# Putting the weight split ahead of older work in the order of two engines

## The chip, the cores and the metric

The kernel runs on one core of one Trainium2 chip. The metric is device time in microseconds of one execution; lower is better.

## The reference

One layer of a model step, on a prompt of 512 tokens and 64 sample tokens (8 requests of 8), with float32 data. A combined projection of the normalised input feeds three branches, and the merged result goes through an output projection:

```python
hn = _rmsnorm(x, norm_g)
u, v, gate_a, z, xbc, dt_raw, q, gate_x, merge = split(hn @ w_in)
h_a = gelu(u) * spatial(layernorm(gelu(v))) * silu(gate_a)
xs, bm, cm = split(silu(causal_conv(xbc)))            # SSD branch
y, h_new = ssd(xs, softplus(dt_raw + dt_bias), -exp(a_log), bm, cm, h0)
h_b = gated_group_rmsnorm(y + d_skip * xs, z, ssd_norm_g)
h_x = mem_attention(q, mem_k, mem_v) * silu(gate_x)
m = g_a * (h_a @ w_proj_a) + g_b * (h_b @ w_proj_b) + g_x * (h_x @ w_proj_x)
return x + m @ w_out
```

The SSD branch is a state-space recurrence in chunks of 128 tokens, with 32 heads in 8 groups. The change lies in the stage that computes this branch.

## The kernel before

Tokens lie along the free dimension: 576 columns, the 512 of the prompt and the 64 samples, in two halves of 288. To multiply float32 data, every operand is split in two: `hi` is a rounded copy, `lo` is the difference. A product of 128 output rows is then three chains of matmuls per half, hi x hi, hi x lo and lo x hi, 24 matmuls of 288 columns per half (line 167).

The weights of a product are split right before use. `load_block` (line 130) reads a block of raw weights for two products into `wraw` (two buffers) on SyncE's queue. `wsplit` makes `whi` by a cast on ScalarE (line 98) and `wlo` by a subtraction on VectorE (line 99); both have two buffers. So the split of a product needs the buffers of the product two before it, and these are free when TensorE has done the last matmul of that one.

The SSD stage is a list of 72 such products, each a `Job` with three parts: `load`, `prep` (the split) and `half`, which runs for each half and also empties the PSUM buffer:

- `conv_job`: rows of xBC. The half is copied out of PSUM by ScalarE (lines 404, 408, 409), then a convolution of four taps follows, one on ScalarE (416) and three on VectorE (418), a tanh (420) and the gate, which makes `xs` or `C` (422, 426, 429); GpSimd copies a part of xs (432).
- `z_job`: the gate z. A tanh on ScalarE (462), then a multiplication on VectorE that reads the same PSUM buffer and makes `zs` (463).
- `gate_job`: merge gates, a tanh (732).
- `proj_job`: products of the finished branch (`hb`) with 512 rows of w_proj_b; a job makes two output row blocks, each in two blocks of 12 matmuls with a PSUM buffer of its own, added into `m_sb` on VectorE (755).

Three PSUM buffers (`acc`) serve all of these, in turn. Group g's jobs are the four conv products of group g + 1 (in the last group four gate products), two z products of group g and, from group 2 on, two proj products; four gate and eight proj products end the stage. In even groups from 2 on the order is conv, conv, conv, conv, z, proj, z, proj; in odd groups from 3 on conv, proj, conv, proj, conv, conv, z, z.

Between the halves stand the steps of the recurrence of group g, written out by hand in `steps(g)`: decays (e: 488, 489, 491), transposes and dt weighting (503 to 511), C x B (532, 533), the diagonal part (548, 559), the state (567 to 574), its part of the output (592 to 597), the sample states (644 to 659), and the gated norm of the group before (`gate_y`, `norm_y`: 685 to 705, with Ln in 701). They use the PSUM buffers `sps` (three) and `yps` (two). What a step leaves in PSUM is read by ScalarE or VectorE, and the buffer is free for a later step when that is done.

What sets the order: TensorE's instructions run as they are written (`manual_schedule`). For the other engines a planner steps through a modelled run of the program and gives each engine, whenever it is free, that ready instruction which has the lowest number. An instruction's number is counted up as the code is written. The result is a fixed queue for each engine, which it works through in order. The loop that writes the products:

```python
for j, h in units:
    ...
    i = at[id(j)]
    if h == 0:
        if i + 2 < len(jobs):
            jobs[i + 2].load()
        if i + 1 < len(jobs):
            jobs[i + 1].prep()
    j.half(h)
```

So at the start of a product the split of the next one is written, behind all steps written so far and ahead of the current product's own evacuations.

Of the kernel before, what the change touches and what calls it, by code (L numbers as in the profile page):

```python
# [42 lines left out]
def tile_hybrid_step(  # L43
# [156 lines left out]
    with ExitStack() as stb:  # L200
# [562 lines left out]
        with tc.manual_schedule(engines={mybir.EngineType.PE}):  # L763
# [63 lines left out]
            jobs = [u[0] for u in units if u[0] is not None and u[1] == 0]  # L827
# [4 lines left out]
            for j, h in units:  # L832
                if j is None:
                    for w_ in h:
                        w_()
                    continue
                i = at[id(j)]
                if h == 0:
                    if i + 2 < len(jobs):
                        jobs[i + 2].load()  # L840
                    if i + 1 < len(jobs):
                        jobs[i + 1].prep()
                j.half(h)

    lo_last[0] = True
# [648 lines left out]
```

## Time and profile before

| | |
|---|---|
| median of 3 runs | 1150.23 us (1148.32 to 1156.42) |
| profiled execution, its own time | 1151.22 us |
| span of the profiled execution | 1149.5 us |
| TensorE busy (PE) | 1099.6 us, 96% of the span |
| VectorE busy (DVE) | 781.9 us, 68% |
| ScalarE busy (ACT) | 622.1 us, 54% |
| GpSimd busy (POOL) | 37.7 us, 3% |

The span goes from the first to the last instruction of the program. Busy time is the union of an engine's instructions; a matmul's end is modelled, so neighbouring matmuls overlap by a little. The SSD stage runs from the start of the kernel to about 646 us. In the rows PE is TensorE's matmuls, PEld its weight loads, SPq SyncE's queue, and L99 line 99 of the kernel.

### The profile page before, as it was taken

The page shows a single profiled execution, that of the slowest core. Times are in us where ns is not written, and L with a number is a line of the kernel's source. Part 1 is how long each engine was busy: PE and PEld are TensorE (multiplying, and loading weights), DVE is VectorE, ACT ScalarE, POOL GpSimd, SP SyncE. Part 2 cuts the span into 40 slices and gives each one's busy share as a digit, 9 for nine tenths or more (in the row PEclk, how much of TensorE's full clock was granted, in tenths as well). Part 3 has the DMA queues.
Part 4 walks back from the last instruction along what each step waited for, and adds up shares of the span by engine and source line. Part 5 has one row for each costly group of instructions (what it writes and reads, how often), then busy time and mean ns, then how long its engine had stood idle before and what let it go on. Part 6 is the DMA issues. An engine that isn't in the chain of part 4 may idle for free.

```text
span 1149.5 us, 20445 instructions
## 1 busy us (share of the span) xinstructions
PE 1099.6 (96%) x8199; PEld 1024.1 (89%) x8199; DVE 781.9 (68%) x1450; ACT 622.1 (54%) x1294; POOL 37.7 (3%) x110
## 2 busy tenths in 40 slices
PE   5989999899999989989999999999999999999997
PEld 4989899799998989989999877899999999889776
DVE  5778787748787667866644644786875567775743
ACT  6456686766868456665553244344653236564421
POOL 3010010000000000000000000000000000000000
PEclk9999999999999999999999999999999999999999
DMA  6433544155352524425232525631262353465411
GB/s 190 128 82 111 156 116 138 59 159 145 98 156 84 155 88 126 126 70 169 88 115 95 190 74 165 193 111 52 96 222 101 130 180 102 121 183 197 152 47 73
DMA packets 160462, 144.90 MB, mean 126 GB/s; under 512 B 10160, under 2 KB 141264, under 8 KB 160368
## 3 DMA queue, kind: packets, MB, share of 16 engines
q1 hardware_dynamic: 137264, 126.12, 35.9%
q10 hardware_dynamic: 23104, 17.49, 4.8%
q8 instruction: 64, 1.05, 0.4%
q14 instruction: 30, 0.25, 0.1%
HBM read 124.13 MB, written 19.46 MB: 125 GB/s over the span
## 4 chain that ended last, share of the span: by engine, by line
PE 84%; DVE 6%; ACT 5%; DMA 3%; issue 1%; ACTq 0%; SPq 0%
PE acc L167 32%; PE acc L908 15%; PE acc L154 12%; PE acc L1038 4%; PE acc L1443 4%; PE acc L1103 2%; PE yps L548 2%; DVE cacc L418 1%; PE sps L644 1%; DVE wlo L99 1%; PE sps L503 1%; PE sps L567 1%; PE sps L592 1%; PE yps L674 1%; PE yps L1391 1%
## 5 line engine op out<-in xcount | busy, mean ns | idle before, releaser
L167 PE MATMUL acc<-hn_hi,whi 128*128 128x288 f32 x896 | 272.6, 304 | 1.0 <-ACT thm L732 0.8
L167 PE MATMUL acc<-hn_hi,wlo 128*128 128x288 f32 x896 | 266.2, 297 | 4.1 <-DVE wlo L99 4.1
L167 PE MATMUL acc<-hn_lo,whi 128*128 128x288 f32 x896 | 265.7, 297 | 0.0
L167 PEld LDWEIGHTS acc<-hn_hi,wlo 128*128 128x128 f32 x896 | 169.7, 189 | 4.4 <-DVE wlo L99 4.3
L167 PEld LDWEIGHTS acc<-hn_hi,whi 128*128 128x128 f32 x896 | 170.1, 190 | 3.6 <-ACT thm L732 1.0
L167 PEld LDWEIGHTS acc<-hn_lo,whi 128*128 128x128 f32 x896 | 170.0, 190 | 0.5
L98 ACT CAST w<-wraw 128x1024 fp32r<-128x1024 f32 (+1 forms) x64 | 59.2, 942 | 103.4 <-PE acc L908 24.0
L99 DVE TENSOR_TENSOR wlo<-wraw,whi 128x1024 fp32r<-128x1024 f32 x72 | 87.9, 1221 | 31.8 <-ACT whi L98 31.3
L167 PE MATMUL acc<-hb,whi 128*128 128x288 f32 x512 | 105.2, 301 | 3.1 <-DVE zs L463 2.6
L98 ACT CAST whi<-wraw 128x1024 fp32r<-128x1024 f32 x72 | 75.5, 1049 | 56.1 <-PE acc L167 48.3
L99 DVE TENSOR_TENSOR w<-wraw,w 128x1024 fp32r<-128x1024 f32 x64 | 68.5, 1087 | 36.0 <-ACT w L98 35.9
L908 PE MATMUL acc<-hn_hi,w 128*128 128x288 f32 x512 | 89.5, 300 | 0.0
L908 PE MATMUL acc<-tT,w 128*128 128x288 f32 x576 | 86.1, 298 | 0.0
L167 PEld LDWEIGHTS acc<-hb,whi 128*128 128x128 f32 x512 | 82.7, 191 | 3.7 <-DVE zs L463 2.8
L418 DVE SCALAR_TENSOR_TENSOR cacc<-raw,cwh,cacc 128x600 f32<-128x600 f32 x96 | 80.3, 838 | 4.2 <-ACT cacc L416 3.7
L908 PEld LDWEIGHTS acc<-tT,w 128*128 128x128 f32 x576 | 78.5, 188 | 0.9 <-issue 0.9
L167 PE MATMUL acc<-hb,wlo 128*128 128x288 f32 x256 | 76.0, 297 | 2.8 <-DVE wlo L99 2.8
L908 PEld LDWEIGHTS acc<-hn_hi,w 128*128 128x128 f32 x512 | 74.1, 188 | 2.1 <-DVE thx L926 0.5
L491 ACT ACTIVATE e<-e,nacs 128x128 f32<-128x128 f32 (+1 forms) x160 | 50.3, 386 | 16.4 <-DVE e L489 16.4
L99 DVE TENSOR_TENSOR w<-S,w 128x1024 fp32r<-128x1024 f32 x32 | 39.2, 1224 | 25.1 <-ACT w L98 25.1
L167 PEld LDWEIGHTS acc<-hb,wlo 128*128 128x128 f32 x256 | 48.8, 191 | 3.1 <-DVE wlo L99 3.1
L154 PE MATMUL acc<-ha,w 128*128 128x288 f32 x384 | 51.5, 295 | 0.0
(392 smaller groups left out, 2137.6 us busy)
## 6 DMA issues: line engine op xcount, KB each, us to landing
wraw<-in_w_in_dram SPq DMA_DIRECT2D x44, 1024.0 KB
wraw<-in_w_in_dram SPq DMA_DIRECT2D x16, 512.0 KB
e<-a_scr SPq DMA_DIRECT2D x32, 256.0 KB
h<-in_state_ssm_dram SPq DMA_DIRECT2D x16, 512.0 KB
out_dram<-h ACTq DMA_DIRECT2D x16, 512.0 KB
wraw<-in_w_proj_b_dram SPq DMA_DIRECT2D x8, 1024.0 KB
ebc<-e_scr SPq DMA_DIRECT2D x16, 288.0 KB
wraw<-in_w_mem_kv_dram SPq DMA_DIRECT2D x4, 1024.0 KB
```

The lines of the kernel that those rows point to most:

```text
L98: S.copy(hi, v)
L99: (e or V).tensor_tensor(lo, v, hi, ALU.subtract)
L154: PE.matmul(ps[:n, :width], lhsT=a, rhs=b[:, sl], start=(i == 0), stop=(i == last))
L167: PE.matmul(ps[:, 0:HT], lhsT=a[:, k], rhs=b(k)[:, sl], start=(n == 0), stop=(n == 3 * nk - 1))
L418: V.scalar_tensor_tensor(a[:, 0:n], raw[:, i:i + n], cwh[:, i, q:q + 1], a[:, 0:n], ALU.mult, ALU.add)
L491: S.activation(e[:, h, 0:w], e[:, h, 0:w], AF.Exp, bias=nacs[:, c, h0_ + h:h0_ + h + 1])
L503: PE.transpose(tp[:, j * P:(j + 1) * P], xs[:, j, c0:c0 + P], ident)
L548: m = PE.matmul(y4[64 * r:64 * r + 64, i, j], lhsT=xdt[:, h], rhs=e[:, h, 0:w], start=True, stop=True)
L908: PE.matmul(ps[:, 0:HT], lhsT=w[:, r, k], rhs=x(q, k), start=first and n == 0, stop=n == 11, skip_group_check=True)
L1038: PE.matmul(pss[i], lhsT=x(k)[:, c], rhs=w[:, r, k2], start=(k + q == 0), stop=(k == KD - 1 and q == 2))
L1103: PE.matmul(pss[i], lhsT=x[xr], rhs=w[:, r, k2], start=(k + q == 0), stop=(k == KD - 1 and q == 2))
L1443: PE.matmul(ps[:, 0:cn], lhsT=x(k)[:, c], rhs=w, start=(k + q == 0), stop=(k == KD - 1 and q == 2))
```

## The change

The split of the next product is written inside a block that sets the counter of the instruction numbers back by 160; behind the block the count goes on as before. The load ahead of it and the half behind it are outside the block.

```diff
                     if i + 2 < len(jobs):
                         jobs[i + 2].load()
                     if i + 1 < len(jobs):
-                        jobs[i + 1].prep()
+
+                        with tc.high_priority(160):
+                            jobs[i + 1].prep()
                 j.half(h)
```

## Rows read from the trace of the kernel before

**Rows 1.** The page: busy time of each engine, and the chain by engine.

```profile
PE 1099.6 (96%) x8199; PEld 1024.1 (89%) x8199; DVE 781.9 (68%) x1450; ACT 622.1 (54%) x1294; POOL 37.7 (3%) x110
...
PE 84%; DVE 6%; ACT 5%; DMA 3%; issue 1%; ACTq 0%; SPq 0%
```

**Rows 2.** Busy time by stretch: PE, PEld, DVE, ACT, POOL, granted clock, DMA.

```profile
45.00:645.00 600.00, 574.19 (x4594) 551.60 (x4593) 428.58 (x831) 379.85 (x885) 27.28 (x87) 0.99 0.41 122
```

**Rows 3.** Waits from 45 to 645 us: in total, times, longest.

```profile
ACT whi L98 <- PE acc L167: 48.3, 25, 5.4
...
PE acc L167 <- DVE wlo L99: 6.9, 2, 4.1
...
PE acc L699 <- DVE m_sb L755: 3.7, 1, 3.7
...
PE acc L167 <- DVE zs L463: 2.6, 1, 2.6
...
PE sps L503 <- DVE h L659: 2.2, 2, 1.1
...
PE sps L592 <- DVE hT L574: 1.7, 3, 1.0
```

**Rows 4.** Groups of ScalarE, 45 to 645 us: busy, mean ns, idle before.

```profile
L98 ACT CAST whi<-wraw 128x1024 fp32r<-128x1024 f32 x69 | 72.4, 1050 | 49.7 <-PE acc L167 48.3 <-DMA wraw<-in_w_in_dram 1.3
```

**Rows 5.** Order of time, 80 to 120 us: start, duration, instruction.

```profile
82.45 1.06 ACT L98 CAST whi<-wraw 128x1024 fp32r<-128x1024 f32 x1
...
83.90 1.22 DVE L99 TENSOR_TENSOR wlo<-wraw,whi 128x1024 fp32r<-128x1024 f32 x1
...
91.27 0.38 PE L167 MATMUL acc<-hn_hi,whi 128*128 128x288 f32 x1
```

**Rows 6.** Order of time, ScalarE, VectorE and TensorE, 201 to 216 us.

```profile
201.69 0.35 ACT L408 COPY raw<-acc 128x224 f32<-128x224 f32 x1 [0.75 <-PE acc L167]
...
207.98 1.03 ACT L98 CAST whi<-wraw 128x1024 fp32r<-128x1024 f32 x1
...
214.28 1.23 DVE L99 TENSOR_TENSOR wlo<-wraw,whi 128x1024 fp32r<-128x1024 f32 x1
...
215.56 0.61 PE L167 MATMUL acc<-hn_hi,wlo 128*128 128x288 f32 x1 [4.10 <-DVE wlo L99]
```

**Rows 7.** Busy time by stretch; the granted clock follows POOL.

```profile
215.42:218.83 3.41, 3.27 (x13) 3.28 (x14) 3.38 (x9) 2.21 (x6) 0.00 (x0) 0.50 0.02 5
...
359.50:361.30 1.80, 1.71 (x12) 1.62 (x12) 1.80 (x6) 0.98 (x3) 0.00 (x0) 1.00 0.03 9
...
502.14:505.55 3.41, 3.41 (x17) 3.41 (x16) 3.38 (x8) 0.94 (x2) 0.00 (x0) 0.50 0.00 0
```

**Rows 8.** Order of time, VectorE and TensorE in group 4.

```profile
359.08 0.46 DVE L463 SCALAR_TENSOR_TENSOR zs<-th,acc 128x288 f32<-128x288 f32 x1
...
359.59 0.40 PE L167 MATMUL acc<-hb,whi 128*128 128x288 f32 x1 [2.57 <-DVE zs L463]
```

**Rows 9.** Order of time, VectorE and TensorE in group 6.

```profile
500.24 1.23 DVE L99 TENSOR_TENSOR wlo<-wraw,whi 128x1024 fp32r<-128x1024 f32 x1
...
502.21 0.82 DVE L463 SCALAR_TENSOR_TENSOR zs<-th,acc 128x288 f32<-128x288 f32 x2
...
501.52 0.40 PE L167 MATMUL acc<-hb,wlo 128*128 128x288 f32 x1 [2.84 <-DVE wlo L99]
```

**Rows 10.** Order of time, TensorE and ScalarE behind group 0.

```profile
120.25 0.52 PE L503 MATMUL sps<-ident,xs 128*128 128x128 f32 x3 [1.08 <-DVE h L659]
...
125.54 1.05 ACT L98 CAST whi<-wraw 128x1024 fp32r<-128x1024 f32 x1
```

**Rows 11.** Waits of SyncE's own queue, 80 to 560 us.

```profile
SPq L130 <- DVE wlo L99: 121.1, 21, 24.7
```

**Rows 12.** Lines 99 and 432: ns min/median/max, first and last start.

```profile
L99 DVE TENSOR_TENSOR wlo<-wraw,whi x72: 1210/1220/1228, 22.1 to 634.5; 128x1024 fp32r<-128x1024 f32 x72
...
L432 POOL COPY xs<-xs x24: 296/694/1568, 54.5 to 493.6; 128x128 f32<-128x128 f32 x24
```

## The prediction

> **What bounds the kernel now.** I read the page's busy times and chain first. TensorE is busy 96% of the span and holds 84% of the chain that ended last [rows 1], so only a change in TensorE's waits, or in its clock, can move the time. The second view is the table by stretches: in the stretch that the change touches, 45 to 645 us, TensorE is busy 574.19 of 600 us [rows 2]. The rest of the span hangs on this stretch through TensorE, so what is won or lost passes to the end. All that any reordering of VectorE and ScalarE can win there is 25.8 us, plus what a lower clock adds inside the busy time. The third view is the list of waits of that stretch: which engine waited for which line, in total, how often, and the longest. TensorE waits for the split itself (the subtraction of line 99) only twice, 6.9 us together; its other waits are for evacuations and state steps: zs, m_sb, h, hT [rows 3]. The reader is to see that the split is late for two products of some seventy, and that what the split would be put in front of is what TensorE waits for elsewhere.
>
> **What the change does to the order.** An instruction gets its number as it is written; the planner gives each engine the lowest-numbered instruction that is ready. The change takes 160 off the numbers of two instructions per product: the cast to whi on ScalarE (1050 ns) [rows 4] and the subtraction to wlo on VectorE (1220 ns) [rows 12]. In this stretch the trace holds 4594 + 831 + 885 + 87 instructions for 69 splits [rows 2, 4], about 93 per product, so 160 reaches some 1.7 products back (an estimate from these counts): the pair goes ahead of nearly everything pending. It cannot go ahead of its own releases: whi and wlo have two buffers, so the split of the next product is ready when the last matmul of the product before the current one is done. No instruction and no DMA is added, and no work leaves either engine; TensorE's order is written by hand and stays. The split issues no DMA, so nothing of it moves on SyncE's queue, and nothing of it is on GpSimd's.
>
> **Where it costs and gains nothing.** A usual product: cast at 82.45, subtraction 83.90 to 85.12, first matmul that needs them from 91.27 [rows 5]: over 6 us of cover. Moving such a split earlier gains 0. The work it jumps is late by 1.05 us on ScalarE or 1.22 on VectorE, until the place where the split stood; after that the engine is where it was before. It costs TensorE only where a jumped instruction has less cover than that. The subtraction also frees the raw weights' buffer: SyncE's weight loads stood 121.1 us waiting for it [rows 11]. These loads will start earlier. The casts wait for TensorE's line 167, not for loads [rows 3], so that gains 0; getting in front of other loads on the same queue could cost, but among TensorE's waits none is for a load, so I put it at 0 as well.
>
> **Gain A, the first z product of group 2.** Its buffer is free at about 201.65 (the evacuation at 201.69 starts on the same matmul), its cast runs at 207.98, its subtraction from 214.28, and TensorE stands 4.10 us at 215.56 [rows 6]. Directly behind, the granted clock is 0.50 for 3.41 us, 1.2 instead of 2.4 GHz [rows 7], which is half of 3.41 = 1.71 us of lost work. With the cast at 201.7 and the subtraction by 204, both go: 4.10 + 1.71 = 5.81 us.
>
> **Gain B, the first proj product of group 6.** TensorE stands 2.84 us at 501.52 for a subtraction that starts at 500.24 [rows 9], and the clock is again 0.50 for 3.41 us [rows 7]: 2.84 + 1.71 = 4.55 us. A and B together are 10.36 us.
>
> **What is late next at A and B.** The second block of 12 matmuls of the first proj product needs the PSUM buffer that line 463 (zs) empties. In group 4, where no split is late, exactly that costs 2.57 us [rows 8]. For A I give back these 2.57 (bounds: 0, and 2.57 + 1.22 + 1.71 if the next split also goes in front of zs). For B: TensorE stood from 501.52 - 2.84 = 498.68 with 10 of the 12 matmuls to do; 12 take 1.71 [rows 7], so 10 take 1.43 and the buffer is wanted at 500.1. The two zs run from 502.21, so the first is done at about 502.62 (half of 0.82 later) [rows 9]; without the subtraction ahead of it that is 501.39: a wait of 1.3, or 2.5 if the next product's subtraction is put in that place. I take 1.9. Kept: (5.81 - 2.57) + (4.55 - 1.9) = 5.9 us, bounds 0 and 10.36.
>
> **Losses.** C, group 4: the zs at 359.08 stands behind VectorE's convolution work, and the split of the second z product becomes ready before it. Put in front, it adds 1.22 to the 2.57 wait, 3.79 in all. After 2.57 the clock stayed at 1.00, after 2.84 it fell [rows 7 to 9]; so I add 1.71 for the clock: 2.93 us (bounds 0, and 3.98 if ScalarE's part comes late by its 1.05 too). D, ends of groups 0 and 1: TensorE waits twice, 2.2 us, for h (line 659) [rows 3], which needs ScalarE's scalings of line 658; the cast now stands behind that work, at 125.54, and goes in front of it: 2 x 1.05 = 2.1 us (bounds 0 and 2.1) [rows 10]. E, state steps: line 592 waits three times for hT, at most 1.0 us [rows 3], so there is no cover left; each can grow by 1.22. Whether the subtraction is ready in time to pass them no row shows: bounds 0 and 3.7; I take two of the three, 2.4 us. Sum of losses 2.93 + 2.1 + 2.4 = 7.4 us, bounds 0 and 9.8.
>
> **The sum.** -5.9 + 7.4 = +1.5 us on the profiled execution's own 1151.22 us (span 1149.5 and 1.7 around it), 1152.7. That execution is 1.0 above the median of the runs shown, 1150.23; on the median it is 1151.7, which I give as 1152.
>
> A second engine works beside the subtraction. GpSimd's copy of xs (line 432) took 296 ns at the least and 1568 at the most, the subtraction 1210 to 1228 ns in all its 72 runs [rows 12]: of these two only the copy gets longer. By the rows the move costs TensorE 0 here. The Trainium skill, SBUF — State Buffer, section Who interferes with whom, says that a VectorE instruction with two SBUF inputs and a GpSimd instruction that reads SBUF exclude each other, and the second to start waits for the first. The trace agrees where the copy is second (1568 against 296 ns); that a subtraction waited for a copy no row shows. By that rule a subtraction that moves right behind a running copy would stand up to 0.30 us, at A, B and C together 0.9, and the sum would be +2.4 in place of +1.5.
>
> **Rivals.** *All gain, no loss*: the jumped work has the cover, zs comes in time. Then -10.36: 1139.9. If the m_sb wait of 3.7 [rows 3] goes as well, with another 1.71 for its clock drop (an estimate by the drop behind A), it is -15.7: 1134.5, the only way past 1%. For it: ScalarE is busy 380 and VectorE 429 of 600 us [rows 2]. Against: TensorE's waits fall just where these engines are dense. *Slower*: the evacuation that stands behind the split becomes the bound. The mechanism is one: the split is ready in the moment that a product's last matmul is done, which is also when that product's evacuation and the state steps become ready; each queue runs in order, so a wait of ScalarE on the cast (25 times already, 48.3 us, longest 5.4) holds all that is behind it [rows 3]. Its places are the ends of seven groups (the h wait of line 503) and the norm steps of seven groups (the m_sb wait of line 699, for a PSUM buffer) [rows 3]: 14 x 1.22 = 17.1 us; and the zs before the first proj product of groups 2, 4 and 6, with the clock: 3 x (1.22 + 1.71) = 8.8. Less the 10.36 gained this is +15.5, 1166. It decides for slower by over 1% from about 22 of these 25.9 us on, that is, when nearly every place pays the full subtraction; four or five of them are in my forecast. *It does nothing*: at the two late products the planner's own times hold the cast by something else than older work (the load, the buffer), and elsewhere the split was first already, as 25 casts with ScalarE idle before them suggest [rows 3]. Then no wait moves: 1150.
>
> **How the numbers follow.** Forecast, gains and losses within a few us of each other, 1152: 0.52. All gain: 0.18, of which 0.07 lies beyond 1%. Nothing: 0.18, inside 1%. Slower mechanism in most places: 0.12, almost all beyond 1%; the forecast's own upper bound (no gain kept, all losses, +9.8) adds 0.01. A change of 1% is 11.5 us, about what a measurement can tell here: the three runs of before lie from 1148.32 to 1156.42. So faster 0.07, same 0.80, slower 0.13. The range reaches from the all-gain case, 1140, to 1163, within the slower mechanism, and leaves out the 0.07 beyond the one end and 0.1 beyond the other.
>
> **What would show it.** Right: TensorE's waits for wlo are gone, the casts that wait for line 167 rise from 25 to well over 40, the drops of the clock behind 215 and 501 are gone, and the waits of line 167 for zs are longer or more. Wrong: TensorE still waits for wlo (the order did not move); or the stage ends over 10 us earlier, with the waits for zs and h no longer than now (C to E mis-sized); or many new waits for raw, zs, e and hT, in every group, with more than four drops of the clock.

## The result, and the profile after

The changed kernel takes 1162.31 us (median of 8 runs, 1158.82 to 1165.88) against 1150.49 us for the kernel before (8 runs, 1148.32 to 1156.87): a ratio of 1.0096, with a 95% interval from 1.0078 to 1.0113. By the medians it is slower by 11.8 us, by the ratio by 11.0; 1.5 us was forecast. The profiled execution of after is the lowest of its runs, 1158.82 us (span 1157.1), 7.60 above that of before. The two profiles can explain these 7.6 and not the rest of the 11.8: the other seven executions of after are slower than the profiled one, and their mean granted clock is lower too (0.982 to 0.992, against 0.993).

Page of after, busy time of each engine and the chain by engine:

```profile
PE 1103.2 (95%) x8199; PEld 1024.3 (89%) x8199; DVE 780.7 (67%) x1450; ACT 627.8 (54%) x1298; POOL 34.2 (3%) x110
...
PE 80%; DVE 8%; ACT 6%; DMA 3%; issue 2%; ACTq 0%; SPq 0%; DVEq 0%
```

Beside [rows 1], TensorE's share of the chain fell from 84 to 80%, and VectorE and ScalarE took over what it lost. One number looks harmless and is the key: ScalarE has 1298 instructions where it had 1294, and 5.7 us more of busy time. A change of order should add none. The stretch of [rows 2] in after, with the same columns:

```profile
45.00:645.00 600.00, 570.43 (x4549) 544.71 (x4548) 423.86 (x824) 385.89 (x890) 22.80 (x87) 0.99 0.41 118
```

TensorE gets 45 fewer matmuls done in these 600 us, and ScalarE is busy 6.0 us longer.

Waits of after, TensorE from 45 to 660 us, then ScalarE and SyncE's queue in the windows of [rows 3, 11]: in total, times, longest.

```profile
PE sps L592 <- ACT hb L98: 5.2, 1, 5.2
...
PE acc L167 <- DVE zs L463: 3.2, 2, 1.6
...
PE sps L592 <- DVE hT L574: 2.1, 4, 0.8
...
PE acc L167 <- DVE wlo L99: 1.2, 3, 0.4
```

```profile
ACT whi L98 <- PE acc L167: 52.5, 29, 5.4
```

```profile
SPq L130 <- DVE wlo L99: 159.6, 11, 29.6
```

TensorE's waits for the split shrank from 6.9 us to 1.2. At the top stands one new wait of 5.2 us at line 592. Line 99 holds the weight loads of SyncE's queue no shorter (159.6 us, fewer but longer waits, against 121.1). The prediction had them start earlier; these waits show nothing of it, and no wait for a load reached TensorE.

To see where the time went I compared the products one by one: the length of a product is the time from its first matmul of line 167 to that of the next. These lines stand for most of the difference (us):

| product | before | after | change | forecast |
|---|---|---|---|---|
| group 1, fourth conv | 8.64 | 14.51 | +5.87 | 0 |
| group 1, first z | 9.19 | 10.95 | +1.76 | 0 |
| group 2, first z (A) | 12.87 | 7.20 | -5.67 | -5.81 |
| group 2, first proj (behind A) | 8.27 | 11.19 | +2.92 | +2.57 |
| group 4, first proj (C) | 11.11 | 11.68 | +0.57 | +2.93 |
| group 6, first z and first proj (B) | 21.26 | 18.85 | -2.41 | -2.65 |
| last of group 0 and of group 1 (D) | 24.21 | 25.17 | +0.96 | +2.1 |

The stage ends at 653.51 instead of 646.24 us, 7.27 later, of which 0.92 was there before its first product. The first two rows are 7.63 us, as much as the whole difference. No term of the prediction's sum stood there.

ScalarE in group 1, in order of time: first the kernel before, then after.

```profile
149.79 1.28 ACT L701 ACT_TABLE_LOAD   x1
151.09 0.71 ACT L701 ACTIVATE zs<-acc 128x288 f32<-128x288 f32 x2
...
152.10 1.28 ACT L702 ACT_TABLE_LOAD   x1
153.40 0.69 ACT L702 ACTIVATE zs<-zs 128x576 f32<-128x576 f32 x1
153.99 0.24 ACT L627 CAST bst<-sps 96x128 fp32r<-96x128 f32 x1
```

```profile
149.89 1.28 ACT L701 ACT_TABLE_LOAD   x1
151.18 0.41 ACT L701 ACTIVATE zs<-acc 128x288 f32<-128x288 f32 x1
...
152.39 1.28 ACT L491 ACT_TABLE_LOAD   x1
153.69 1.07 ACT L491 ACTIVATE e<-e,nacs 128x64 f32<-128x64 f32 x4
154.77 1.28 ACT L701 ACT_TABLE_LOAD   x1
156.07 0.41 ACT L701 ACTIVATE zs<-acc 128x288 f32<-128x288 f32 x1
...
156.78 1.28 ACT L702 ACT_TABLE_LOAD   x1
158.08 0.68 ACT L702 ACTIVATE zs<-zs 128x576 f32<-128x576 f32 x1
...
158.96 0.25 ACT L627 CAST bst<-sps 96x128 fp32r<-96x128 f32 x1
```

Line 701 is the Ln of the norm step, one for each half of the columns; lines 702 and 491 are Exp. Whenever ScalarE goes from the one function to the other, a table load of 1283 ns stands in front. Before, the two Ln came together and the four Exp of line 491 ahead of them: two loads. After, these Exp fell between the two Ln: four loads. From the first load to the end of line 702 it is 4.3 us before and 8.87 after, and line 627, which reads a PSUM buffer, starts 4.97 us later. The two added loads are 2.57 us of that and the four Exp, which now run inside the norm step, 1.07. What follows on VectorE and TensorE in after:

```profile
158.79 0.82 DVE L705 SCALAR_TENSOR_TENSOR ysb<-ysb,gh,zs 128x576 f32<-128x576 f32 x1 [4.46 <-ACT zs L702]
...
162.20 0.29 DVE L628 TENSOR_TENSOR bst<-sps,bst 32x128 fp32r<-32x128 f32 x1
```

```profile
162.64 1.19 PE L592 MATMUL sps<-C,hT 128*128 128x128 f32 x4 [5.15 <-ACT hb L98]
```

```profile
161.69:168.52 6.83, 5.52 (x22) 5.26 (x23) 6.65 (x17) 4.60 (x12) 0.49 (x3) 0.50 0.31 84
```

VectorE idles 4.46 us for line 702; line 628, which empties the buffer that line 592 writes next, comes behind that, and TensorE stands 5.15 us. The trace names the cast of `hb`, which ended 162.61; line 628 ended 0.12 earlier, and in the kernel before it is the one that releases line 592. In the last row (busy time by stretch) the granted clock is 0.50, 1.2 in place of 2.4 GHz, for 6.83 us, from the last microsecond of the wait on: up to 3.4 us more.

How often, by the groups of ScalarE's instructions from 45 to 655 us (busy, mean ns, idle before), before and then after:

```profile
L701 ACT ACT_TABLE_LOAD x10 | 12.8, 1283 | 0.2
...
L702 ACT ACT_TABLE_LOAD x7 | 9.0, 1283 | 0.1
...
L491 ACT ACT_TABLE_LOAD x3 | 3.8, 1283 | 0.1
```

```profile
L701 ACT ACT_TABLE_LOAD x12 | 15.4, 1283 | 0.2
...
L702 ACT ACT_TABLE_LOAD x8 | 10.3, 1283 | 0.1
...
L491 ACT ACT_TABLE_LOAD x4 | 5.1, 1283 | 0.1
```

Eight norm steps need eight first loads for Ln. Ten means that an Exp stands between the two Ln in two of them (groups 4 and 6); twelve, in four (now 1 and 2 as well). Four more loads of 1.283 are 5.1 of ScalarE's 5.7 us.

### The profile page after: what moved, and what is told of

It reads as the page before. It is cut to its first block, busy times and chain, and to the rows that moved or that the text cites. A ratio compares the mean times of both kernels' runs of the same rounds, so it can differ in the third digit from the quotient of the medians.

```text
span 1157.1 us, 20484 instructions
## 1 busy us (share of the span) xinstructions
PE 1103.2 (95%) x8199; PEld 1024.3 (89%) x8199; DVE 780.7 (67%) x1450; ACT 627.8 (54%) x1298; POOL 34.2 (3%) x110
## 3 DMA queue, kind: packets, MB, share of 16 engines
q8 instruction: 64, 1.05, 0.4%
## 4 chain that ended last, share of the span: by engine, by line
PE 80%; DVE 8%; ACT 6%; DMA 3%; issue 2%; ACTq 0%; SPq 0%; DVEq 0%
PE acc L167 31%; PE acc L910 14%; PE acc L154 12%; PE acc L1040 4%; PE acc L1445 4%; PE acc L1105 2%; DVE cacc L418 2%; PE yps L548 1%; DVE wlo L99 1%; ACT whi L98 1%; DMA e<-a_scr 1%; PE sps L644 1%; ACT e L491 1%; PE sps L503 1%; PE sps L592 1%
## 5 line engine op out<-in xcount | busy, mean ns | idle before, releaser
L910 PE MATMUL acc<-hn_hi,w 128*128 128x288 f32 x512 | 89.5, 300 | 0.2 <-DVE g L928 0.2
L154 PE MATMUL acc<-hn_hi,w 128*128 128x288 f32 x256 | 51.2, 295 | 0.0
```

What stands on the lines that cost most here:

```text
L154: PE.matmul(ps[:n, :width], lhsT=a, rhs=b[:, sl], start=(i == 0), stop=(i == last))
L910: PE.matmul(ps[:, 0:HT], lhsT=w[:, r, k], rhs=x(q, k), start=first and n == 0, stop=n == 11, skip_group_check=True)
```

## The experiments

**Theory 1:** the loss is these table loads: the new order lets an Exp in between the two Ln of a norm step, above all in group 1. **Theory 2:** it is the sum of many small delays of the work that the 71 splits are put in front of, as the prediction's terms C to E had it, only in more places. Ratios are against the kernel before on the same chip, with 95% intervals.

**Both Ln kept together in group 1 alone.** The changed kernel, and in line 701:

```diff
-                S.activation(rs[:, sl], ms[:, 0:HT], AF.Ln)
+                with ExitStack() as up:
+                    if g == 0:
+                        up.enter_context(tc.high_priority(200))
+                    S.activation(rs[:, sl], ms[:, 0:HT], AF.Ln)
```

> The changed kernel, with the two Ln of one norm step alone (that of group 0, run in group 1) put ahead in ScalarE's order, so that no Exp comes between them. Theory 1, table loads: in the changed kernel four Exp and two more table loads stand between these two Ln, TensorE waits 5.15 us behind them and then has 6.83 us at half clock (3.4 us of work); this alone is most of what was lost. Then 7 to 8 us below the changed kernel's 1162.3: 1154 to 1156, with the 5.15 us wait of line 592 gone. Theory 2, the sum of many small delays of evacuations and state steps as forecast (C to E): the place is one of many, no more than 2 us: 1160 to 1162.

Measured: 1159.76 us, ratio 1.0077 (1.0056 to 1.0099). In the waits from 140 to 180 us the one of line 592 is left with 2.1 of its 5.15:

```profile
PE sps L592 <- DVE bst L628: 2.1, 1, 2.1
PE sps L503 <- DVE t L595: 1.7, 1, 1.7
```

In place theory 1 is right: the two products of group 1 win 4.38 and 1.77, 6.2 together, and no half clock follows. But three products beside them (third conv and second z of group 1, first conv of group 2) are 3.9 us longer than in after, and the median fell by 2.5 only; the intervals of the two ratios overlap. It lies between the two expectations, below theory 2's and above theory 1's. One removed cause uncovers the next; so far both theories hold a part.

**Both Ln kept together in every norm step**, in the changed kernel and in the kernel before:

```diff
-                S.activation(rs[:, sl], ms[:, 0:HT], AF.Ln)
+                with tc.high_priority(200):
+                    S.activation(rs[:, sl], ms[:, 0:HT], AF.Ln)
```

> The changed kernel, with the two Ln of all eight norm steps kept together. Theory 1: 12 table loads before Ln become 8, ScalarE has about 10 us less to do (4 x 2.57), the stretches around groups 1, 2, 4 and 6 get shorter: 1148 to 1153, at or below the kernel before. Theory 2: the small delays stay: 1158 to 1162.

> The kernel before with the two Ln of all norm steps kept together, the split left where it was. Theory 1: it too has two norm steps with an Exp between the Ln (groups 4 and 6), 2 x 2.57 us of ScalarE; TensorE's waits there (2.57 in group 4, 1.09 and 2.84 with a clock drop of 1.71 in group 6) shrink: 1143 to 1148. Theory 2: table loads lie beside TensorE's path: 1149 to 1151.

Measured: after, paired, 1155.78 us, ratio 1.0046 (1.0030 to 1.0062); before, paired, 1146.84 us, 0.9964 (0.9946 to 0.9982). The loads in front of Ln (line 702 in these two) go to eight in both, and all loads of the stage to 16, from 24 and 20. The kernel before came out as theory 1 had it, the kernel after between the two theories. Pairing is worth 5.8 us to the kernel after (0.50% of 1150) and 4.1 to the kernel before. So with no mixed Ln in either, the change still costs 0.82%, 9.4 us: theory 2 is needed for that. Waits of after, paired:

```profile
PE sps L503 <- DVE t L595: 7.2, 4, 1.9
...
PE sps L503 <- DVE h L659: 4.2, 3, 2.3
```

Line 595 and line 659 read PSUM buffers on VectorE, and the buffers come free late. At all four waits for line 595 VectorE's queue shows why: the moved subtraction stands in front of line 595 with line 489 between them, and it had itself waited 0.17 to 0.36 us for its cast. The first of the four:

```profile
148.19 1.23 DVE L99 TENSOR_TENSOR wlo<-wraw,whi 128x1024 fp32r<-128x1024 f32 x1 [0.17 <-ACT whi L98]
149.33 0.42 DVE L489 TENSOR_TENSOR e<-e,tri 128x256 f32<-128x256 f32 x1
149.66 0.42 DVE L595 TENSOR_TENSOR t<-sps,ebc 128x256 f32<-128x256 f32 x1
```

```profile
150.23 0.52 PE L503 MATMUL sps<-ident,xs 128*128 128x128 f32 x3 [1.71 <-DVE t L595]
```

That is theory 2 at work. The kernel before, paired, has two such waits of line 503 for line 659 (2.2 us) and none of note for line 595. In it the waits A, B and C are gone although no split was moved: the products of [rows 6, 8, 9] are shorter by 5.84, 2.83 and 4.63 us. So the late split was a follow-up of the norm step in front of it. But the edit does two things: it keeps the two Ln together, and it puts both ahead of older work. In group 2, at A, the kernel before had its two Ln together already; no load is saved there, and the new plan has the cast at 205.06, ahead of the norm step, where before it stood behind it at 207.98. The 4.1 and 5.8 us are the worth of the edit, not of the loads alone.

**Priority for the two late splits alone.**

```diff
-                        jobs[i + 1].prep()
+                        if i + 1 in (20, 53):
+                            with tc.high_priority(160):
+                                jobs[i + 1].prep()
+                        else:
+                            jobs[i + 1].prep()
```

> The kernel before with the split put ahead for the two late products alone, the first z of group 2 and the first proj of group 6. Both theories: the gains without the losses. In the profiles the changed kernel won 5.67 us at the first and gave back 2.92 behind it, and won about 2.4 around the second: 5 us in all, 1144 to 1147. If a rearranged order brings a new wait even so, 1149 or more: then it is any shift of the plan that costs, not the number of splits moved.

Measured: 1147.38 us, ratio 0.9962 (0.9944 to 0.9979). Gains A and B are real (-5.84 and -4.63 at their products, 5.81 and 4.55 in the prediction), and part is given back near by: the two products ahead of A are longer by 2.29 and 1.17, the one ahead of B by 1.51.

**An Exp between the two Ln, with no split moved.** The kernel before, in which only the second Ln is put ahead, so that the plan mixes groups 1, 2, 4 and 6 as in after (and, as after does not, the last norm step, whose two Ln have a tanh between them: 26 loads in the stage in place of 24):

```diff
-                S.activation(rs[:, sl], ms[:, 0:HT], AF.Ln)
+                with ExitStack() as up:
+                    if f == 1:
+                        up.enter_context(tc.high_priority(200))
+                    S.activation(rs[:, sl], ms[:, 0:HT], AF.Ln)
```

> The kernel before with no split moved; only the second Ln of each norm step has an earlier number, and the plan that comes of it has Exp between the two Ln in groups 1, 2, 4 and 6, as the changed kernel has (before: groups 4 and 6 alone). It is the table loads without the moved splits. Theory 1 (the extra loads and the Exp between the Ln are most of the loss): 4 to 8 us slower than before, 1155 to 1159, with a wait of several us of line 592 in group 1. Theory 2 (many small delays by jumped work): 1150 to 1152.

Measured: 1166.43 us, ratio 1.0125 (1.0094 to 1.0157). This is the clearest case for theory 1: without one moved split the wait in group 1 is back, and the half clock behind it (the last row: window, then the engines, clock 0.50).

```profile
164.82 1.20 PE L592 MATMUL sps<-C,hT 128*128 128x128 f32 x4 [5.25 <-DVE bst L628]
```

```profile
163.65:170.48 6.83, 5.66 (x24) 5.69 (x25) 6.66 (x17) 4.98 (x14) 0.48 (x3) 0.50 0.00 0
```

The two products there are longer by 5.27 and 1.98 us, 7.25 (after: 7.63). Not all of that is the loads: in the kernel before, paired, where the Ln are moved as well but not mixed, the first of the two is longer by 1.76 too. The two kernels differ in these two products by 5.5 us, and that is the price of the mixing alone. The whole came out above what theory 1 expected: other products are longer too, for instance the first proj of group 2 by 3.08 and those beside the last norm step by 1.55 and 2.54, and the profile has more drops of the clock, two of them ahead of the first norm step.

**Half of the split.** In `wsplit` the cast and the subtraction are written apart, and only one of them inside the block of 160:

```diff
-        split(raw[:, :, o:o + n], hi, lo, e)
+        S.copy(hi, raw[:, :, o:o + n])
...
+        (e or V).tensor_tensor(lo, raw[:, :, o:o + n], hi, ALU.subtract)
```

> Only the cast to whi has the earlier number, the subtraction keeps its own. The plan has Exp between the Ln in groups 1, 2, 4 and 6. Theory 1: as slow as the changed kernel, 1159 to 1162. Theory 2: ScalarE is the less dense of the two, so the smaller part of the small delays: 1152 to 1155.

> Only the subtraction to wlo has the earlier number, the cast keeps its own. In the plan group 1 keeps its two Ln together, groups 2, 4 and 6 do not. Theory 1: near the kernel before, 1150 to 1154, as the late product of group 2 gains little when its cast stays behind. Theory 2: VectorE is the denser engine and frees the PSUM buffers of the state steps, so the larger part of the loss is here: 1156 to 1160.

Measured: cast alone 1161.46 us, 1.0074 (1.0050 to 1.0097); subtraction alone 1164.48 us, 1.0109 (1.0076 to 1.0142). With the cast ahead, groups 1, 2, 4 and 6 are mixed, line 592 waits 4.6 us and the time is that of theory 1. With the subtraction ahead, group 1 is not mixed (eleven loads), the long wait isn't there, and it is no faster for that: theory 1 expected 1150 to 1154, and it lies above theory 2's 1156 to 1160 as well. In group 1 the two products of the table are still longer by 3.07 and 1.54. The two halves cost more, added up, than the whole split does. Its waits (in these two kernels line numbers are 8 higher; L175 is line 167, L141 line 98, L575 line 567, L519 line 511, L540 line 532, L582 line 574):

```profile
PE acc L175 <- ACT whi L141: 4.4, 3, 1.5
PE sps L575 <- ACT BT L519: 4.3, 2, 2.8
...
PE sps L540 <- DVE hT L582: 2.3, 1, 2.3
```

That is theory 2 nearly by itself: TensorE now waits for casts, transposes and states, and in groups 1, 4 and 6, where all but one of these waits stand, no table load was added; the third wait for a cast is in group 2, which is newly mixed.

**Which products.** Priority from product 24 on, and up to product 23:

```diff
-                        jobs[i + 1].prep()
+                        if i + 1 >= 24:
+                            with tc.high_priority(160):
+                                jobs[i + 1].prep()
+                        else:
+                            jobs[i + 1].prep()
```

> The split goes ahead only for products 24 to 71, that is from group 3 on; the first 24 products are as before. In the profile of the changed kernel the products up to 23 lost 8 us and those behind them won 1.6. Theory 1: groups 1 and 2 are as before, so 1148 to 1151. Theory 2: two thirds of the moved splits remain, and the loss with them, less the gain at the late product of group 6: 1154 to 1157.

> The kernel before with priority for the splits of the first 24 products alone (up to the middle of group 2's product list); the other 48 are written where they were. The norm steps of groups 1 and 2 again have an Exp between their two Ln. Theory 1, the loss is the table loads there and TensorE's wait and half clock behind them: these products carry nearly all of the loss, 1158 to 1162 us, with the wait of some 5 us for line 592 at about 162 us and 6.8 us of half clock. Theory 2, many small delays of jumped work, spread evenly over the 71 moved splits: a third of the loss, 1153 to 1156.

Measured: the later 48 products 1155.06 us, 1.0027 (1.0005 to 1.0049); the first 24 1161.51 us, 1.0087 (1.0065 to 1.0109) (`i + 1 < 24`; these products end with group 2, not in its middle as the expectation says). One third of the moved splits carries nearly all the loss, as theory 1 wanted, and the two thirds that add no table load still cost 3 us, which is in theory 2's range and above theory 1's. The waits of the kernel with the first 24 repeat those of after:

```profile
PE sps L592 <- ACT hb L98: 5.2, 1, 5.2
...
PE acc L167 <- DVE wlo L99: 3.3, 2, 2.8
...
PE acc L167 <- DVE zs L463: 2.5, 1, 2.5
```

Product for product it is the table above: +5.88 and +1.89 in group 1, -5.66 at A, +2.92 behind it, and nothing at B and C, whose waits (2.8 and 2.5) are those of before. In the later kernel's profile the products behind 23 add up to 0.1 us; the 3 us of its median are not seen there.

**A shorter reach.** The changed kernel, both Ln together, and the splits ahead by 40 numbers in place of 160:

```diff
-                        with tc.high_priority(160):
+                        with tc.high_priority(40):
```

> The changed kernel with both Ln of every norm step together, and the splits put ahead by 40 numbers in place of 160, that is past less than half a product's work. With 160 this was 1155.8 us, 9 us above the kernel before with the same pairing. Theory 2, what is left of the loss is the older work that the splits are put in front of: with less of it jumped most of the 9 us goes, 1147 to 1151 us. Theory 1, only table loads cost and these 9 us have another source: no change, 1154 to 1157.

Measured: 1152.87 us, ratio 1.0014 (0.9996 to 1.0032). Of the 9.4 us that remained with pairing, 3.7 go with the shorter reach (1.0046 to 1.0014), and the four waits for line 595 at line 503 with them; 5.8 remain. Both expectations miss: theory 2 has the direction, but not the size. What is left shows in part. The waits for line 595 did not all go, three now stand at line 644, in the first proj products of groups 2, 4 and 6:

```profile
PE sps L644 <- DVE t L595: 4.0, 3, 1.3
PE sps L592 <- DVE bst L628: 3.6, 1, 3.6
```

These three products are longer by 1.19, 1.57 and 1.52 us than in the kernel before, paired, and the fourth conv and the first z of group 1, where line 592 waits, by 1.27 and 1.54.

**Both remedies.** The kernel before with the two late splits moved and the Ln together:

> The kernel before with priority for the splits of the two late products alone (the first z product of group 2 and the first proj product of group 6) and both Ln of every norm step next to each other. Theory 1: pairing (4.1 us won alone) and the two moved splits (4.4 us won alone) remove the same two waits, so together they win little more than either: 1145 to 1147 us. If the two gains are separate they add: 1142 to 1144.

Measured: 1148.72 us, ratio 0.9967 (0.9949 to 0.9985). Together they win no more than either alone (0.9964, 0.9962): at A and B they remove the same waits (-5.84 and -4.63 in all three). These three are the versions that beat both kernels, by 0.3 to 0.4%.

## Why the prediction held in its range and missed the mechanism

The measured 1162.3 us lies inside the stated range of 1140 to 1163, 0.7 us below its upper end, and the ratio of 1.0096 just inside the 1% that had 0.80, though its interval reaches beyond (1.0113). That is luck more than foresight: the time forecast was 1152, and the upper end stood for evacuations held behind the split in nearly every place. What filled it first was something that no term and no rival had.

**The step that failed** is in the part on the order: "No instruction and no DMA is added, and no work leaves either engine". From it followed "The work it jumps is late by 1.05 us on ScalarE or 1.22 on VectorE, until the place where the split stood; after that the engine is where it was before." On ScalarE that is not so. A new order of Ln and Exp made four more table loads, and in group 1 line 627 was late by 4.97 us in place of 1.05. Where it was, TensorE paid 7.63 us in two products. The experiments without a moved split put the mixing at 5.5 us of that; the cast alone brings the mixing and costs 7.89 there, the subtraction alone costs 4.61 there without it, so jumped work has a part in this place too. The trace of before had these loads in its list of ScalarE's groups, two mixed groups among them, and I priced none of them.

**Gain A** held: 5.67 against 5.81, and the drop of the clock behind 215 went. Cast and subtraction of that product now run some 10 us ahead of its first matmul (215.48), and no wait stands there:

```profile
204.89 1.04 ACT L98 CAST whi<-wraw 128x1024 fp32r<-128x1024 f32 x1
...
205.96 1.28 DVE L99 TENSOR_TENSOR wlo<-wraw,whi 128x1024 fp32r<-128x1024 f32 x1
...
215.48 0.38 PE L167 MATMUL acc<-hn_hi,whi 128*128 128x288 f32 x1
```

**Behind A** 2.92 us came back (forecast 2.57), but in three waits, the longest 1.08 for `m_sb` at line 753, not for zs. **Gain B** with its give-back is right in the sum by luck: -2.41 against -2.65. At the first proj product itself it is -1.24; the other -1.16 is in the z product ahead of it, where a wait of line 532 for hT (1.09 us in the kernel before) went, which no term had. The wait for the late subtraction fell from 2.84 to 0.38 us, the drop of the clock behind 501 is gone, and the wait that gives some back is the one foreseen, for zs:

```profile
515.06 0.54 PE L167 MATMUL acc<-hb,whi 128*128 128x288 f32 x2 [1.58 <-DVE zs L463]
```

**Loss C** did not come: 0.57 in place of 2.93. The zs wait of group 4 is shorter than the 2.57 of [rows 8], beside two small ones, and the clock stayed at 1.00:

```profile
373.94 0.40 PE L167 MATMUL acc<-hb,whi 128*128 128x288 f32 x1 [1.58 <-DVE zs L463]
```

The 1.71 us for the clock in C rested on 2.57 us of waiting that left it at 1.00 and 2.84 that did not. The length of that one wait does not decide: with the cast alone a wait of 2.33 us in the same product is followed by half clock, as this row by stretch shows.

```profile
374.35:377.76 3.41, 3.41 (x24) 2.80 (x23) 3.41 (x8) 1.76 (x5) 0.25 (x2) 0.50 0.02 5
```

**Loss D** did not come as told: line 503 still waits 1.08 for line 659 behind group 0, and behind group 1 it waits 1.7 for line 440; the two products are longer by 0.96 in all. **Loss E** is small: waits of line 592 for hT went from 1.7 to 2.1 us. So of 7.4 us of losses some 2 came where I had put them, and others, 2.4 us net by the profile in pieces from -1.36 to +1.02, spread over the rest of the stage.

**The signs.** The waits for wlo are nearly gone (6.9 to 1.2 us), the drops of the clock behind 215 and 501 are gone, and the waits of line 167 for zs are more (2.6 us in one, 3.2 in two). But the casts that wait for line 167 rose from 25 to 29, not over 40: in most places the order around the cast did not become what I took it for. **GpSimd**: the subtraction took 1211 to 1276 ns in after, the copy of line 432 up to 1605. The longest subtraction is the one at A (205.96, above). It began while a copy of line 432 was running, with 0.20 us of that left, and took 0.05 us more than the longest of [rows 12]. So by the durations the rows' 0 was nearer than the estimate of 0.9 by the rule of the Trainium skill (SBUF — State Buffer, Who interferes with whom). **The rival** that ended slower, evacuations held behind the split, is in part theory 2, yet its places (`m_sb` at the norm steps) were not the ones, and the norm step cost through ScalarE's tables.

**What stays open.** With both Ln together the change still costs 9.4 us by the ratios. The subtraction in front of line 595, the subtraction alone and the shorter reach show that jumped work is behind a part of it. Of the 5.8 us that remain with the shorter reach the products above name some 7 us of losses, against which other products are shorter; which of them make the median is not shown, nor where the 3 us of the later 48 products lie, whose profile shows no such loss. How much of the worth of pairing is the loads, and how much the earlier place of the Ln, no run separates outside group 1.

## What to carry to other kernels

Before an order is changed on an engine that evaluates functions, count its table loads and see which pairs of equal functions the order keeps together; a reordering that adds no instruction to the code can add loads to the queue. Priority is worth giving to the instructions that the trace shows late (two here, -0.38%), not to the whole class (71 here, +0.96%). And ask why the late one is late: here the waits went away as well by an edit of the norm step alone, with the split left where it was.

## What the runs showed of the hardware

Executions of the same instructions differed, and the clock shows where. From 47.15 to 50.56 us, where in the kernel with the later 48 splits moved nothing is moved yet, its profile shows 0.50, and that of before 1.00, with TensorE busy throughout both (window, then the engines, clock):

```profile
47.15:50.56 3.41, 3.41 (x16) 3.38 (x16) 1.77 (x4) 2.39 (x5) 0.35 (x2) 0.50 0.47 121
```

```profile
47.15:50.56 3.41, 3.41 (x27) 3.25 (x26) 3.09 (x6) 2.32 (x5) 0.00 (x0) 1.00 0.72 186
```

It does 16 matmuls in place of 27 there. A profiled execution stood up to 4.3 us from the median of its kernel (1153.02 against 1148.72 with both remedies), which is why sums over one profile were compared here product by product.
